# A one-core decoder trunk in split fp32: warm-up products ordered first, the bias table moved behind the first key product, the sub-norm's mean in another bank, and two output products fed tile by tile

## The chip, the cores and the metric

The kernel runs on one core of a Trainium2 chip. The metric is the time of one execution on the device, in microseconds (us). Several runs are timed, and one execution is recorded by the hardware profiler. Engine names: TensorE (PE, with PEld for its weight loads), VectorE (DVE), ScalarE (ACT), GpSimd (POOL) and SyncE (SP), which issues the DMA loads and stores.

## The reference

Two decoder layers over 512 tokens of width 1024, all in float32. What matters here, shortened:

```python
for i in range(2):
    hn = rmsnorm(h, norm_mix_g[i])
    # layer 0: 8 stick-breaking heads and 4 differential heads; layer 1: 16 dilated-window heads
    h = h + (even_mixer if i == 0 else odd_mixer)(hn, ...)
    hn = rmsnorm(h, norm_mlp_g[i])
    h = h + square(relu(hn @ w_mlp_up[i])) @ w_mlp_down[i]
    h = h + (p[i] @ w_ple_proj[i]) * sigmoid(rmsnorm(h, norm_ple_g[i]) @ w_ple_gate[i])
return rmsnorm(h, final_norm_g)

# differential head, in even_mixer
sc = q @ k.T * scale + t5_table[bucket(rel)]       # two maps per head, causal
attn = softmax(sc[0]) - lam * softmax(sc[1])       # lam from the four lambda vectors
o_d = rmsnorm(attn @ v, subln_g, 1e-5) * (1 - lambda_init)   # the "sub-norm", over 128 values
o = concatenate([o_sb, o_d]); return o @ w_out
```

## The kernel before

**Split products.** Activations lie transposed: h is eight tiles of 128 channels x 512 tokens. Each float32 operand is split into a high and a low half (ScalarE copies the high half, VectorE or GpSimd subtracts to get the low one), and `mm3` (L135 to L138) multiplies high x high, high x low and low x high. Where the page writes mm<-hi,wh or mm<-lo,wh, these are such products.

**Who sets the order.** The code is traced as one long list. A planner at compile time then lays it out on the engines: each engine gets a fixed order, chosen by a simulated clock and by the place in the list, and waits are put in for data and for buffers. On the chip an engine runs its own order strictly and stands still where its next instruction isn't ready. `order(later, earlier)` adds an edge to the plan between two instructions without a wait on the chip. Buffers are rotated by tags: `ps("mm")` has three PSUM banks, "sc" and "tp" two each, "pv" one (`PS_BUFS`). The tile "tmp" has one buffer, the raw weights two, the split weights three.

**Start.** L286 to L309: an activation table is loaded, ten products of the identity with itself (`WARM`, L291, 20 records, to a bank of "mm") are traced as warm-up, and SyncE loads the norm gains, the eight tiles of h and, in three pieces between them, the first weight block (the queries of the first group, `blk0`). Each tile of h is split with its gain (L178, L179) and so is each piece of the block (L308, L309).

**Mixer.** `project(g, cur)` makes queries, keys and values of a group; `attend` does the group's attention as a list of steps; `interleave` traces the steps of one group between the products of the next. Layer 0 takes the groups 2, 3, 0, 1, and 2 and 3 are the differential ones. In the first group `queries_keys` (L443) multiplies both query tiles at once, the eight tiles of h in turn, into two "sc" banks, and leaves the results there (`waiting`). Then it calls `prepare()` (L314), which builds the bias table: seven small loads into "bias" and "tmp" tiles, four small products L329 to "pv" and "tp" banks, four VectorE operations L331, four stores L332 to `urow` in device memory, from which `load_bias` (L511) reads each head's diagonal; it also makes the lambda factor. Then come the key block (load L114, splits L122 and L128) and its two products. After the first of them `statistics()` sums the squares of h (L237, L243), forms the mean with two products (L250, L251) and the reciprocal root (L206 to L212), and with it the held queries and then the keys are evicted (`evacuate`, L470 to L486).

**Attention.** A step scores one block of 128 queries (`scores`, L502, L503), adds the bias and takes the minimum (L519), exponentiates (L522), and with a lag transposes (L528), splits the transposed weights (L536, L537) and, once per head, multiplies with the values into the "pv" bank (`pv`, L547; evicted by L601 or L608). In a differential group `subnorm` follows two steps after each head: squares (L614, L615, L616), the mean over the head's channels by two products L618 and L619 into a "pv" bank, the reciprocal root (L206 to L212, of which L206 and L211 read that bank), and the scaling L621. There are two heads in each of two groups, so four sub-norms.

**Output.** `out_first` multiplies the first six of the eight head tiles with the output weights, beside the attention of the last group: eight sums, each of 18 products in a row into one "mm" bank, added to h by L658. The tiles are split by L175 and L176. Then the last two tiles follow, the MLP, and the per-layer embedding.

Of the kernel before, what the change touches and what calls it, by code (L numbers as in the profile page):

```python
# [19 lines left out]
P = 128  # L20
# [42 lines left out]
def trunk(  # L63
# [5 lines left out]
    nc = tc.nc  # L69
# [28 lines left out]
    def ps(tag):  # L98
        return psum.tile([P, S], F32, tag=tag, name=nm(tag), bufs=PS_BUFS[tag])
# [31 lines left out]
    def block(src, nk, n):  # L131
        raw = wload(src)
        return [wsplit(raw, i, nk, n) for i in range(src.shape[-1] // (nk * n))]

    def mm3(acc, lh, ll, rh, rl, start, stop):  # L135
        nc.tensor.matmul(acc, lh, rh, start=start, stop=False)  # L136
        nc.tensor.matmul(acc, lh, rl, start=False, stop=False)  # L137
        nc.tensor.matmul(acc, ll, rh, start=False, stop=stop)  # L138

# [5 lines left out]
    def lin_units(accs, ws, ahl, k0, nk, outer):  # L145
        pairs = [(i, k) for k in range(nk) for i in range(len(accs))] if outer else \
            [(i, k) for i in range(len(accs)) for k in range(nk)]
        for i, k in pairs:
            ah, al = ahl[k0 + k]
            mm3(accs[i], ws[i][0][:, k], ws[i][1][:, k], ah, al, k == 0, k == nk - 1)  # L150
            yield 2.0
# [31 lines left out]
    ident = const([P, P], "ident")  # L183
# [36 lines left out]
    def order(later, earlier):  # L220
        tc.add_manual_dep(
            later, earlier.name,
            mybir.DependencyInfo(mybir.DependencyClass.NoSync, mybir.DependencyReason.DATA),
            reason="activation tables")
# [63 lines left out]
    nc.scalar.preload_act_table_set("natural_log_exp_and_others")  # L288
    warm = ps("mm")
    for _ in range(WARM):  # L290
        nc.tensor.matmul(warm[:, 0:P], ident, ident, start=True, stop=True)  # L291
    norm = Norm(0, 0)
    raw0 = wpool.tile([P, 2 * KT * P], F32, tag="raw", name=nm("raw"), bufs=2)
    raw0v = raw0.rearrange("p (i k c) -> p i k c", i=2, k=KT)
# [73 lines left out]
    def mixer(layer, norm, nxt):  # L368
# [35 lines left out]
        def project(g, cur):  # L404
            kind = "dil" if layer else ("sb" if g < 2 else "diff")
            start = not first
            first.append(g)
            v = mpool.tile([P, QT, 512], F32R, tag="v", name=nm("v"), bufs=2)

            def values():  # L410
                raw = wload(next_block())
                banks = [ps(lead_in.pop(0)) if start else ps("mm") for _ in range(QT // 2)]
                accs = [b[:, c:c + 256] for b in banks for c in (0, 256)]
                for half in range(2):
                    wh, wl = wsplit(raw, half, 4, 256)
                    if half and "rcol" not in stat:
                        stat["rcol"] = tok_cols(stat["rstd"])
                    for t in range(QT):
                        for k in range(4):
                            ah, al = ahl[4 * half + k]  # L420
                            tk = slice(t * P, (t + 1) * P)
                            mm3(accs[t], ah[:, tk], al[:, tk], wh[:, k], wl[:, k],
                                half == 0 and k == 0 and t % 2 == 0, half == 1 and k == 3 and t % 2 == 1)
                            yield 1.0
                        if half == 1 and t % 2 == 1:
                            evacuate_values(t - 1, accs[t - 1])
                            evacuate_values(t, accs[t])

            def evacuate_values(t, acc):
                sc = stat["rcol"][:, t:t + 1]  # L430
                if kind == "diff":
                    src = acc
                    vh, vl = v[:, t, 0:256], v[:, t, 256:512]
                else:
                    src = acc.rearrange("p (a c) -> p a c", a=4)
                    vv = v[:, t, :].rearrange("p (a b c) -> p a b c", a=4, b=2)
                    vh, vl = vv[:, :, 0, :], vv[:, :, 1, :]
                nc.scalar.activation(vh, src, AF.Copy, scale=sc)
                nc.vector.scalar_tensor_tensor(vl, src, sc, vh.bitcast(F32), op0=ALU.mult, op1=ALU.subtract)

            heads = []

            def queries_keys():  # L443
                qscale = -0.5 * HD ** -0.5 if kind == "sb" else 0.5 * HD ** -0.5
                qk, waiting = [], []
                for isq in (True, False):
                    src = next_block()
                    lo_eng[0] = nc.vector if start else nc.gpsimd
                    blk = blk0 if isq and start and not layer else block(src, KT, P)
                    lo_eng[0] = nc.gpsimd  # L450
                    accs = [ps(lead_in.pop(0)) if start else ps("mm") for _ in range(2)]
                    if start and isq:
                        yield from lin_units(accs, blk, ahl, 0, KT, True)
                        waiting = accs
                        if not layer:
                            prepare()
                        continue
                    for i, acc in enumerate(accs):
                        yield from lin_units([acc], [blk[i]], ahl, 0, KT, False)
                        if waiting:  # L460
                            statistics()
                            for x, held in enumerate(waiting):
                                evacuate(True, x, held, qk, qscale)
                            waiting = []
                        evacuate(isq, i, acc, qk, qscale)

            def evacuate(isq, i, acc, qk, qscale):
                rstd = stat["rstd"]
                f = t2k("tmp")
                nc.vector.scalar_tensor_tensor(f, acc, qscale if isq else -0.5, rstd, op0=ALU.mult, op1=ALU.mult)  # L470
                lower, upper = slice(0, 64), slice(64, 128)
                if isq:
                    qq = []
                    for a, b in ((lower, upper), (upper, lower)):
                        q = mpool.tile([P, S], F32R, tag="qq", name=nm("qq"), bufs=5)
                        nc.scalar.activation(q[a], f[a], AF.Copy)
                        nc.vector.tensor_tensor(q[b], f[a], q[a].bitcast(F32), op=ALU.subtract)
                        qq.append(q)
                    qk.append(qq)
                else:  # L480
                    for s, (a, b) in enumerate(((lower, upper), (upper, lower))):
                        kl = klz[s][kl_i[0] % KLB]
                        kh = mpool.tile([P, S], F32R, tag="kh", name=nm("kh"), bufs=5)
                        nc.scalar.activation(kh[a], f[a], AF.Copy)
                        nc.scalar.activation(kh[b], f[a], AF.Copy)
                        nc.vector.tensor_tensor(kl[a], f[a], kh[a].bitcast(F32), op=ALU.subtract)  # L486
                        heads.append((qk[i][s], kh, kl))
                    kl_i[0] += 1
            cur.extend((g, kind, v, heads))
            if start:  # L490
                yield from queries_keys()
                yield from values()
            else:
                yield from values()
                yield from queries_keys()
# [55 lines left out]
        def attend(g, kind, v, heads):  # L551
# [59 lines left out]
            def subnorm(x):  # L611
                o = oT[2 * g + x]
                hi, rs, lo = t2k("tmp2", dtype=F32R), t2k("tmp2"), t2k("tmp2", dtype=F32R)
                nc.scalar.activation(rs, o, AF.Square)  # L614
                nc.scalar.activation(hi, rs, AF.Copy)  # L615
                nc.vector.tensor_tensor(lo, rs, hi.bitcast(F32), op=ALU.subtract)  # L616
                mp = ps("pv")
                nc.tensor.matmul(mp, ones_r, hi, start=True, stop=False)  # L618
                nc.tensor.matmul(mp, ones_r, lo, start=False, stop=True)  # L619
                rsqrt(rs, t2k("tmp2"), mp, SUBLN_EPS, eps_s, scale=float(D // P))  # L620
                nc.vector.scalar_tensor_tensor(o, o, gsub, rs, op0=ALU.mult, op1=ALU.mult)  # L621
# [30 lines left out]
        def out_first():  # L652
            ohl.extend(split_tile(oT[k]) for k in tiles[len(ohl):6])
            for c in range(4):
                for i, ws in enumerate(block(w_outa[layer, c], 6, P)):
                    acc = ps("mm")
                    yield from lin_units([acc], [ws], ohl, 0, 6, False)
                    nc.vector.tensor_tensor(h[2 * c + i], h[2 * c + i], acc, op=ALU.add)  # L658

        cur = []  # L660
# [360 lines left out]
```

## Time and profile before

| what | value |
|---|---|
| median of 3 runs | 1309.7 us (1309.18 to 1309.81) |
| profiled execution | 1309.79 us |
| its span, first to last instruction | 1308.0 us |
| granted TensorE clock, mean | 0.998 |
| TensorE busy | 1281.9 us (98%) |
| VectorE busy | 974.1 us (74%) |
| ScalarE busy | 686.3 us (52%) |
| GpSimd busy | 191.2 us (15%) |
| DMA | 133.20 MB, mean 102 GB/s |

A row of the timeline has the start in us, the duration, the engine, the line of the program, the operation, output <- inputs, the shapes and how many were merged; in brackets stands how long the engine stood idle before it and what released it. Matmul durations overlap, so the rate of products is read from the distance of their starts. A row of the waits has who waited for whom, the sum in us, how often, and the longest.

### The profile page before, as it was taken

The page shows a single profiled execution, that of the slowest core. Times are in us where ns is not written, and L with a number is a line of the kernel's source. Part 1 is how long each engine was busy: PE and PEld are TensorE (multiplying, and loading weights), DVE is VectorE, ACT ScalarE, POOL GpSimd, SP SyncE. Part 2 cuts the span into 40 slices and gives each one's busy share as a digit, 9 for nine tenths or more (in the row PEclk, how much of TensorE's full clock was granted, in tenths as well). Part 3 has the DMA queues.
Part 4 walks back from the last instruction along what each step waited for, and adds up shares of the span by engine and source line. Part 5 has one row for each costly group of instructions (what it writes and reads, how often), then busy time and mean ns, then how long its engine had stood idle before and what let it go on. Part 6 is the DMA issues. An engine that isn't in the chain of part 4 may idle for free.

```text
span 1308.0 us, 18566 instructions
## 1 busy us (share of the span) xinstructions
PE 1281.9 (98%) x7256; PEld 1116.8 (85%) x7256; DVE 974.1 (74%) x1623; ACT 686.3 (52%) x1117; POOL 191.2 (15%) x160
## 2 busy tenths in 40 slices
PE   7999999999999999999999999999999999999997
PEld 5978788888998989988889888788899898998876
DVE  7688898778848869845767777887785885994566
ACT  6666868554535334334456666765553443533344
POOL 2432444310000000000024333222000000000001
PEclk9999999999999999999999999999999999999999
DMA  6421323223232322323432222212223223232241
GB/s 214 136 82 49 122 89 137 89 84 110 86 108 97 103 93 96 129 97 107 151 114 95 83 89 79 68 57 93 100 97 121 73 97 129 71 124 97 97 145 65
DMA packets 28040, 133.20 MB, mean 102 GB/s; under 512 B 3312, under 2 KB 4048, under 8 KB 15280
## 3 DMA queue, kind: packets, MB, share of 16 engines
q1 hardware_dynamic: 27952, 132.01, 29.2%
q8 instruction: 57, 0.93, 0.3%
q14 instruction: 31, 0.25, 0.1%
HBM read 125.63 MB, written 6.37 MB: 101 GB/s over the span
## 4 chain that ended last, share of the span: by engine, by line
PE 86%; DVE 8%; ACT 3%; issue 1%; DMA 1%; SPq 0%; ACTq 0%; DVEq 0%
PE mm L137 13%; PE mm L136 13%; PE mm L138 13%; PE sc L137 5%; PE sc L138 5%; PE sc L136 5%; PE tp L138 5%; PE tp L137 5%; PE tp L136 5%; PE pv L138 3%; PE pv L137 3%; PE pv L136 3%; PE pv L547 2%; PE tp L528 2%; PE sc L502 1%; PE sc L503 1%
## 5 line engine op out<-in xcount | busy, mean ns | idle before, releaser
L122 ACT ACTIVATE wh<-raw 128x1024 fp32r<-128x1024 f32 (+1 forms) x168 | 173.5, 1037 | 225.3 <-PE mm L137 94.6
L126 POOL TENSOR_TENSOR wl<-raw,wh 128x512 fp32r<-128x512 f32 (+1 forms) x132 | 178.5, 1373 | 308.8 <-ACT wh L122 303.2
L136 PE MATMUL mm<-hi,wh 128*128 128x512 f32 x548 | 216.2, 395 | 1.0 <-ACT hi L175 0.6
L138 PE MATMUL mm<-hi,wl 128*128 128x512 f32 x548 | 214.3, 391 | 0.8 <-DVE wl L128 0.8
L137 PE MATMUL mm<-lo,wh 128*128 128x512 f32 x548 | 214.4, 391 | 0.2 <-DVE lo L176 0.2
L128 DVE TENSOR_TENSOR wl<-raw,wh 128x1024 fp32r<-128x1024 f32 x102 | 124.4, 1224 | 41.2 <-ACT wh L122 34.8
L138 PEld LDWEIGHTS mm<-hi,wl 128*128 128x128 f32 x548 | 102.9, 188 | 23.8 <-DVE wl L128 1.2
L136 PEld LDWEIGHTS mm<-hi,wh 128*128 128x128 f32 x548 | 103.0, 188 | 20.5 <-ACT wh L122 1.2
L137 PEld LDWEIGHTS mm<-lo,wh 128*128 128x128 f32 x548 | 103.0, 188 | 19.0 <-DVE lo L176 0.5
L522 ACT ACTIVATE e<-e,mn 128x128 f32<-128x128 f32 (+3 forms) x96 | 53.9, 562 | 66.3 <-DVE mn L519 65.9
L745 ACT ACTIVATE wh<-raw 128x1024 fp32r<-128x1024 f32 x48 | 50.7, 1056 | 69.8 <-PE tp L137 35.5
L136 PE MATMUL sc<-hi,wh 128*128 128x512 f32 x184 | 72.3, 393 | 6.4 <-ACT wh L308 6.4
L724 DVE TENSOR_TENSOR ul<-u,uh 128x1792 fp32r<-128x1792 f32 (+1 forms) x32 | 58.4, 1824 | 23.4 <-ACT uh L723 23.4
L723 ACT ACTIVATE uh<-u 128x1792 fp32r<-128x1792 f32 (+1 forms) x32 | 49.4, 1543 | 48.5 <-DVE u L719 48.2
L138 PE MATMUL mm<-uh,wl 128*128 128x256 f32 (+1 forms) x240 | 73.7, 307 | 0.0
L137 PE MATMUL mm<-ul,wh 128*128 128x256 f32 (+1 forms) x240 | 73.5, 306 | 0.0
L136 PE MATMUL mm<-uh,wh 128*128 128x256 f32 (+1 forms) x240 | 72.9, 304 | 0.0
L137 PE MATMUL sc<-lo,wh 128*128 128x512 f32 x184 | 72.2, 392 | 0.0
L138 PE MATMUL sc<-hi,wl 128*128 128x512 f32 x184 | 72.1, 392 | 0.0
L712 ACT ACTIVATE u<-u 128x512 f32<-128x512 f32 x64 | 39.4, 624 | 54.5 <-DVE u L711 54.5
L137 PE MATMUL mm<-wl,hi 128*128 128x256 f32 (+1 forms) x224 | 66.1, 295 | 0.5 <-DVE wl L128 0.5
L136 PE MATMUL mm<-wh,hi 128*128 128x256 f32 (+1 forms) x224 | 66.1, 296 | 0.0
(263 smaller groups left out, 3498.8 us busy)
## 6 DMA issues: line engine op xcount, KB each, us to landing
raw<-in_w_up_dram SPq DMA_DIRECT2D x32, 1024.0 KB, 4.9
raw<-in_w_down_dram SPq DMA_DIRECT2D x32, 1024.0 KB, 4.9
raw<-in_w_in_dram SPq DMA_DIRECT2D x23, 1024.0 KB, 4.9
raw<-in_w_gate_dram SPq DMA_DIRECT2D x8, 1024.0 KB, 4.9
bias<-urow SPq DMA_DIRECT2D x24, 256.0 KB, 3.9
raw<-in_w_outa_dram SPq DMA_DIRECT2D x8, 768.0 KB, 4.3
pj<-pjd SPq DMA_DIRECT2D x16, 256.0 KB, 4.4
h<-in_xT_dram SPq DMA_DIRECT2D x8, 256.0 KB, 5.6
```

Of the source, the lines that this page charges most:

```text
L122: nc.scalar.activation(hi, src, AF.Copy)
L126: nc.gpsimd.tensor_tensor(lo[:, kx], src[:, kx], hi[:, kx].bitcast(F32), op=ALU.subtract)
L128: nc.vector.tensor_tensor(lo, src, hi.bitcast(F32), op=ALU.subtract)
L136: nc.tensor.matmul(acc, lh, rh, start=start, stop=False)
L137: nc.tensor.matmul(acc, lh, rl, start=False, stop=False)
L138: nc.tensor.matmul(acc, ll, rh, start=False, stop=stop)
L522: nc.scalar.activation(e[:, 0:n], e[:, 0:n], AF.Exp, scale=-1.0, bias=mn, accum_out=s)
L528: nc.tensor.transpose(tp[:, j * P:(j + 1) * P], e[:, j * P:(j + 1) * P], ident)
L712: nc.scalar.activation(ui, ui, AF.Square, scale=0.5)
L723: nc.scalar.activation(uh[:, parts], u[:, parts], AF.Copy)
L724: nc.vector.tensor_tensor(ul[:, parts], u[:, parts], uh[:, parts].bitcast(F32), op=ALU.subtract)
L745: nc.scalar.activation(hi, src, AF.Copy)
```

## The change

Four edits. The first key or query product traced gets a planning edge behind the last warm-up product. `prepare()` is called later: not before the key block but after the first key product, the statistics and the evictions of both query tiles. The sub-norm's mean goes to a bank of "mm" instead of "pv". In `out_first` both sums of a weight block take their banks together, and in the first block (c = 0) the six tiles are taken in turn, three products for one sum and three for the other; the additions to h are traced after both sums.

```diff
@@ -132,8 +132,12 @@
+    warm_end = []
+
     def mm3(acc, lh, ll, rh, rl, start, stop):
-        nc.tensor.matmul(acc, lh, rh, start=start, stop=False)
+        mm = nc.tensor.matmul(acc, lh, rh, start=start, stop=False)
+        if warm_end:
+            order(mm.ins, warm_end.pop())
         nc.tensor.matmul(acc, lh, rl, start=False, stop=False)
         nc.tensor.matmul(acc, ll, rh, start=False, stop=stop)
@@ -288,7 +292,7 @@
     warm = ps("mm")
     for _ in range(WARM):
-        nc.tensor.matmul(warm[:, 0:P], ident, ident, start=True, stop=True)
+        warm_end[:] = [nc.tensor.matmul(warm[:, 0:P], ident, ident, start=True, stop=True).ins]
@@ -452,8 +456,6 @@
                     if start and isq:
                         yield from lin_units(accs, blk, ahl, 0, KT, True)
                         waiting = accs
-                        if not layer:
-                            prepare()
                         continue
                     for i, acc in enumerate(accs):
                         yield from lin_units([acc], [blk[i]], ahl, 0, KT, False)
@@ -462,6 +464,8 @@
                             for x, held in enumerate(waiting):
                                 evacuate(True, x, held, qk, qscale)
                             waiting = []
+                            if not layer:
+                                prepare()
                         evacuate(isq, i, acc, qk, qscale)
@@ -614,7 +618,7 @@
-                mp = ps("pv")
+                mp = ps("mm")
                 nc.tensor.matmul(mp, ones_r, hi, start=True, stop=False)
                 nc.tensor.matmul(mp, ones_r, lo, start=False, stop=True)
@@ -652,9 +656,10 @@
             for c in range(4):
-                for i, ws in enumerate(block(w_outa[layer, c], 6, P)):
-                    acc = ps("mm")
-                    yield from lin_units([acc], [ws], ohl, 0, 6, False)
+                blk = block(w_outa[layer, c], 6, P)
+                accs = [ps("mm") for _ in range(2)]
+                yield from lin_units(accs, blk, ohl, 0, 6, c == 0)
+                for i, acc in enumerate(accs):
                     nc.vector.tensor_tensor(h[2 * c + i], h[2 * c + i], acc, op=ALU.add)
```

## The prediction

> **What bounds the kernel now.** I read the page first (busy shares, then the chain that ended last), then the list of waits of TensorE, then the timeline of the stretches in which those waits lie.
>
> ```profile
> PE 1281.9 (98%) x7256; PEld 1116.8 (85%) x7256; DVE 974.1 (74%) x1623; ACT 686.3 (52%) x1117; POOL 191.2 (15%) x160
> ...
> PE 86%; DVE 8%; ACT 3%; issue 1%; DMA 1%; SPq 0%; ACTq 0%; DVEq 0%
> ```
>
> TensorE is busy 98% of the span and is 86% of the chain; VectorE (DVE) has 8% of it. So time can be saved only where TensorE stands still, runs at a slow clock, or does work that nobody needs. The waits say where it stands still:
>
> ```profile
> PE sc L136 <- ACT wh L308: 6.4, 1, 6.4
> PE pv L547 <- DVE tmp L211: 2.8, 2, 1.4
> ...
> PE mm L136 <- ACT hi L175: 0.6, 1, 0.6
> ```
>
> The longest is the first product's wait for its weights, which the change does not touch. The others that bear on the change are 2.8 us in two pieces on a PSUM bank that the sub-norm holds, and 0.6 us before an output product. So what the change can bring is a matter of microseconds in 1308.
>
> The timeline of the start shows work that is slow or useless rather than late:
>
> ```profile
> 1.11 0.29 POOL masks.py:199 TENSOR_SCALAR_AFFINE_SELECT ident<-ident 128x128 f32<-128x128 f32 x1
> ...
> 6.95 0.63 PE L137 MATMUL sc<-lo,wh 128*128 128x512 f32 x1
> ...
> 9.08 0.45 PE L136 MATMUL sc<-hi,wh 128*128 128x512 f32 x1
> 9.37 2.39 PE L291 MATMUL mm<-ident 128*128 128x128 f32 x20
> 11.52 0.47 PE L137 MATMUL sc<-lo,wh 128*128 128x512 f32 x1
> ...
> 20.70 0.39 PE L138 MATMUL sc<-hi,wl 128*128 128x512 f32 x1
> 21.02 1.03 PE L329 MATMUL pv<-prep,prep 32*16 32x512 f32 x2
> 22.32 0.50 PE L250 MATMUL tp<-e,ones_r 128*128 128x512 f32 x1
> 23.26 0.50 PE L136 MATMUL mm<-hi,wh 128*128 128x512 f32 x1 [0.45 <-ACT wh L122]
> ...
> 35.86 0.28 PE L136 MATMUL pv<-wh,hi 128*128 128x256 f32 x1
> ```
>
> Products 2 to 7 start 0.43 us apart ((9.08 - 6.95) / 5); after 11.52 they start 0.23 us apart (40 steps up to 20.70). So the clock rises near 9.08, some 2.7 us after TensorE's first instruction at 6.4. Then the ten warm-up products (20 records) run from 9.37 to 11.52: behind seven real products, when the clock is already up. They cost 2.15 us and warm nothing. Their operand, the identity, was there at 1.40.
>
> **Part 1: warm-up first.** TensorE is idle until 6.4, so the 20 records start at about 1.5. At the fast rate they take 2.15 us, at half of it 4.3; they end between 3.7 and 5.8, before the first weights are split at 6.4. They cost nothing: what hides them is the wait of 6.4 us. If that cover were gone, the price is at most the 2.15 us they cost now. The seven slow products gain 7 x 0.20 = 1.4 us and the moved records 2.15, together 3.55 us if data keeps up. It does not quite:
>
> ```profile
> 12.63 2.07 DVE L179 SCALAR_TENSOR_TENSOR lo<-h,gcols,hi 128x512 fp32r<-128x512 f32 x3
> ...
> 8.10 0.43 SPq L317 DMA_DIRECT2D prep<-in_t_table_dram  x1
> ...
> 14.33 0.82 SPq L114 DMA_DIRECT2D raw<-in_w_in_dram  x2
> ...
> DMA to landing us min/median/max: 5.0/6.0/6.9
> ...
> 14.34 0.72 ACT L178 ACTIVATE hi<-h,gcols 128x512 fp32r<-128x512 f32 x1 [0.58 <-DMA h<-in_xT_dram]
> ...
> 22.17 1.99 ACT L122 ACTIVATE wh<-raw 128x1024 fp32r<-128x1024 f32 x2
> ...
> 24.50 2.34 DVE L128 TENSOR_TENSOR wl<-raw,wh 128x1024 fp32r<-128x1024 f32 x2
> ```
>
> The query products take the tiles of h in turn, six products each. The low halves of tiles 4 to 6 are made from 12.63 on, 0.69 us each, so the first is there at 13.32; from 6.4 the 24 products of the first four tiles need 5.5 us and leave 1.4 us for waits on their own halves. After 13.32 there are 23 products, 5.3 us, and the block ends at 18.6 (tile 7, whose high half starts at 14.34, is in time). Now it ends at 20.93. Gain 2.3 us; ends 1.0 (another half us at each of three tiles) and 3.55.
>
> [...]
>
> **Part 2: the bias table behind the first key product.** Now the seven small loads (first at 8.10) stand in SyncE's queue ahead of the key weights, issued at 14.33, and the key split is behind the statistics on ScalarE (22.17). In the change the key load takes the place of the load at 8.10. The two 1 MB loads issued from 14.33 on, 0.4 us apart, landed 5.0 and 6.9 us after issue, so they are served in line, 2.3 us each: the key weights come 2.3 us behind the last tile of h (there at 14.34), at about 16.6.
>
> Two ScalarE splits of 1.0 us and two VectorE splits of 1.17 us follow, among the squares. First high half about 18, first low half about 19.4. So the key products can begin at 18.6, against 23.26. From 20.93 to 35.86 TensorE now has 48 products (11.0), the two of the statistics (0.46) and the four small table products (21.02 to 22.32, 1.3): 12.8 of 14.9 us, 2.1 idle. The small products move back and still cost their 1.3. Of the idle time I keep 1.1: 0.4 for the first low half, 0.7 because the statistics' products now follow the first key product and their sum is delayed on VectorE by the two key splits (2.3 us). Key products end at 18.6 + 12.8 + 1.1 = 32.5; gain of both parts 35.86 - 32.5 = 3.4 us. Ends: 0 (the key split still planned behind the statistics, and the small products in the way later; a loss would need a key load issued after 14.33, and nothing new stands ahead of it) and 3.55 + 2.1 = 5.65; I take 3.4, from the data rows.
>
> What is moved, queue by queue. SyncE: seven loads go behind one key load (1 MB, 2.3 us); the value load waits for its buffer as now. The four stores of the table wait for VectorE's four small operations, and the bias loads for the stores; the bias is first used behind the first scores, 30 us after the table's products at 21.02. Those four operations leave VectorE's queue in front of the low-half split. The lambda load shares a one-buffer tile with the query and key evictions; if it gets that only behind both queries, the first key eviction is held for a load, less than the 5.0 us of the 1 MB ones. That lies in a slack:
>
> ```profile
> 28.20 0.95 DVE L212 SCALAR_TENSOR_TENSOR rstd<-e,rstd 128x512 f32<-128x512 f32 x1
> ...
> 38.68 0.69 DVE L486 TENSOR_TENSOR klz<-tmp,kh 64x512 fp32r<-64x512 f32 x1 [0.61 <-ACT kh L484]
> ...
> 51.04 0.28 PE L502 MATMUL sc<-kh,qq 128*128 128x256 f32 x1
> ```
>
> The norm is ready at 29.15, the first heads at 39.4, their scores start at 51.04 and would start near 47.6, 8 us after the heads. Both delays fit. So the whole attention stage starts 3.4 us earlier, and its weight loads with it.
>
> **Part 3: the sub-norm's mean in a general bank.** There is one "pv" bank. The sub-norm's mean holds it until VectorE's L211, and the next head's value product waits:
>
> ```profile
> 85.67 0.69 DVE L537 TENSOR_TENSOR ptl<-tp,pth 128x512 fp32r<-128x512 f32 x1
> ...
> 87.84 0.47 PE L547 MATMUL pv<-pth,v 128*128 128x512 f32 x1 [1.40 <-DVE tmp L211]
> 88.14 0.40 PE L547 MATMUL pv<-ptl,v 128*128 128x512 f32 x1
> 88.38 0.56 PE L547 MATMUL pv<-pth,v 128*128 128x512 f32 x2
> ...
> 91.76 0.57 ACT L601 ACTIVATE o<-pv 128x512 f32<-128x512 f32 x1
> ...
> 93.69 0.69 DVE L616 TENSOR_TENSOR tmp<-tmp,tmp 128x512 fp32r<-128x512 f32 x1 [1.77 <-ACT tmp L615]
> ...
> 94.44 0.50 PE L619 MATMUL pv<-tmp,ones_r 128*128 128x512 f32 x1
> ...
> 102.55 0.39 PE L502 MATMUL sc<-kh,qq 128*128 128x256 f32 x1 [1.07 <-DVE mn L519]
> ```
>
> L537, the operand of that product, is ready at 86.4; without the bank the product starts 1.4 us earlier, and as much at the second of the two waits. What is late next: TensorE runs on to the next sub-norm's product L619, which at 94.44 already waits for L616, and that hangs on L601, whose row names no wait: it stood in ScalarE's queue behind the key copies, and was not held by the value product. With that order kept, all of the gain is lost at L619; with L601 moved ahead of the copies, up to 2.8 is kept. After it stands a wait for VectorE at 102.55. I take 0.8, nearer to the kept order; ends 0 and 2.8 (a loss is the fourth rival). Cost: a general bank is held for over six us (below).
>
> **Part 4: first two output products tile by tile.**
>
> ```profile
> 847.00 0.39 PE L136 MATMUL mm<-hi,wh 128*128 128x512 f32 x1
> ...
> 851.37 0.49 PE L136 MATMUL mm<-hi,wh 128*128 128x512 f32 x1 [0.57 <-ACT hi L175]
> 852.10 0.50 PE L137 MATMUL mm<-lo,wh 128*128 128x512 f32 x1 [0.23 <-DVE lo L176]
> ```
>
> In the last layer the first product's sixth tile (15 products after 847.00) waits for its high and its low half, there at 852.1. In turn over two banks 30 products stand ahead of it, until 853.8: the wait goes. 0.57 + 0.23 = 0.8 us, ends 0 and 0.8. TensorE is the bound there, so it is kept; a loss is excluded while the bank count suffices. In the first layer no such wait is listed: nothing. Two banks now finish together; the third carries the next product for 4 us (18 x 0.23) while two additions of 0.7 us free them.
>
> **Sum.** 3.4 + 0.8 + 0.8 = 5.0 us off the profiled execution's 1309.79 (span 1308.0 and 1.8 around it; 0.1 above the median of the runs): 1304.8. Ends of the terms: 0 and 9.25 off, so 1309.8 and 1300.5.
>
> **Rivals.** 1. The front gain is lost: the attention of the first group is paced by VectorE and ScalarE, or the planned order keeps the key split late. For it: the norm is ready at 29 either way, and VectorE holds TensorE up as late as 102.55. Against: the scores start 11 us after their heads. Then only parts 3 and 4 stand, 1.6 off: 1308.2.
>
> 2. The clock is still slow at 6.4: the warm-up is done early, or TensorE's pause before 6.4 lets it fall. Then the first seven products stay slow and 1.4 us of the front go: 1306.2. Against it: after 1.40 us without work, at 87.84, products of 512 columns are again 0.24 us apart (88.14 to 88.38). [...]
>
> 3. More: L601 moves ahead and both sub-norm waits are kept, the front reaches 4.5: 4.5 + 2.8 + 0.8 = 8.1 off, 1301.7.
>
> 4. Slower: three general banks no longer do. The mean takes one from about 94 to the end of L211 at 100.84, the values' products need two at once, and a key sum waits for its eviction:
>
> ```profile
> 95.66 0.69 DVE L470 SCALAR_TENSOR_TENSOR tmp<-mm,rstd 128x512 f32<-128x512 f32 x1 [1.28 <-PE mm L138]
> ...
> 95.47 0.28 PE L136 MATMUL mm<-wh,hi 128*128 128x256 f32 x1
> ...
> 98.33 0.28 PE L136 MATMUL mm<-wh,hi 128*128 128x256 f32 x1
> ...
> 100.17 0.67 DVE L211 SCALAR_TENSOR_TENSOR tmp<-pv,tmp 128x512 f32<-128x512 f32 x1
> ```
>
> If the values' second bank has to be the mean's, TensorE stops from 98.33 to 100.84, 2.5 us, at each of four sub-norms: 10.0 - 4.2 (the sum without part 3) = 5.8 slower, 1315.6. It decides from 1.05 us per sub-norm. Against it: the key sum's bank is free at 96.35, 2 us before it is needed.
>
> **How the numbers follow.** The forecast 0.57 (own range 1302.5 to 1306.8), rival 1 0.17, rival 2 0.07, rival 3 0.11, rival 4 0.08. The time predicted is the likeliest, 1304.8. The range for 8 in 10 is 1301.2 to 1308.6: it drops rival 4 and the far end of rival 3. A change under 0.2% (2.6 us) can't be told from none here: faster, below 1307.1: 0.57 + 0.07 + 0.11 = 0.75; same, 0.17; slower 0.08.
>
> **What will show it.** Part 1: the warm-up rows before 6.36 and query products 0.23 apart from the first; the last near 18.6. Part 2: the key load issued near 8.1, first key product near 18.6, first value product near 32.5, first scores near 47.6. Part 3: no wait of L547 on L211; then L619 or L502 waits longer, or L601 stands ahead of the key copies. Part 4: no wait on L175 and L176 near 847. It is wrong if the stretch from 60 to 145 gives the front gain back, or if waits on a general bank appear: the planned order of all queues is made anew, and a wait of one or two us anywhere in the attention stages weighs as much as any part of this.

## The result: slower by 4 us instead of faster by 5

| kernel | median, us | lowest to highest | ratio to before, 95% |
|---|---|---|---|
| before | 1310.16 (8 runs) | 1309.18 to 1312.15 | |
| after | 1314.16 (8 runs) | 1313.43 to 1316.63 | 1.0029 [1.0019, 1.0040] |

The medians differ by 4.0 us, 0.3%, and the interval of the ratio lies above 1. The forecast was 1304.8, in a range that ended at 1308.6. The page of the changed kernel, busy time and the shares of the chain that ended last:

```profile
PE 1287.3 (98%) x7256; PEld 1119.7 (85%) x7256; DVE 973.0 (74%) x1623; ACT 686.1 (52%) x1117; POOL 188.7 (14%) x160
...
PE 84%; DVE 9%; ACT 5%; issue 1%; DMA 1%; SPq 0%; POOL 0%; ACTq 0%; DVEq 0%; POOLq 0%
```

Its span is 1313.3 us and its granted clock 0.996, against 0.998 before. TensorE is busy 5.4 us longer than before (1287.3 against 1281.9) with the same number of instructions: some of its work ran at a slower clock. In the chain, VectorE and ScalarE gained what TensorE lost: new waits.

To find where time is won and lost, I numbered the products that `mm3` makes in order of their start (6360 in each trace) and took the difference of the n-th starts, after minus before. The columns name the start of that product in before; the first is the first key product, the last is the last product. The two profiled executions took 1315.09 and 1309.79 us, so this table adds up to 5.3 us and not to the 4.0 of the medians.

| kernel | 23.3 | 36.0 | 58.2 | 144.6 | 179.0 | 258.0 | 1299.4 |
|---|---|---|---|---|---|---|---|
| after | -4.1 | -3.2 | -1.0 | -0.1 | +3.2 | +5.1 | +5.3 |

So the front gains 3.2, against 3.4 forecast, and three places take it away and more: the start of the attention (36 to 58, and the rest until 70), a place between 145 and 179, and one between 179 and 258. From 258 to the end the difference grows by only 0.2.

**The front comes out as forecast.** Timeline of TensorE, after:

```profile
1.46 3.93 PE L295 MATMUL mm<-ident 128*128 128x128 f32 x20 [1.46 <-POOL ident masks.py:199]
5.72 0.50 PE L138 MATMUL sc<-hi,wh 128*128 128x512 f32 x1 [0.33 <-ACT wh L312]
6.06 0.40 PE L141 MATMUL sc<-lo,wh 128*128 128x512 f32 x1
6.29 0.42 PE L142 MATMUL sc<-hi,wl 128*128 128x512 f32 x1
...
19.18 0.39 PE L138 MATMUL mm<-hi,wh 128*128 128x512 f32 x1
...
32.62 0.28 PE L138 MATMUL pv<-wh,hi 128*128 128x256 f32 x1
...
47.80 0.28 PE L506 MATMUL sc<-kh,qq 128*128 128x256 f32 x1
...
50.32 0.28 PE L142 MATMUL mm<-wh,lo 128*128 128x256 f32 x1
52.58 0.39 PE L506 MATMUL sc<-kh,qq 128*128 128x256 f32 x1 [1.99 <-DVE mn L523]
```

The warm-up is done at 5.7, the first product is followed at the fast rate, the key products follow the last query product without a pause at 19.18, the first value product stands at 32.62 (forecast 32.5), and the first scores at 47.80 (forecast 47.6). Then the second scores wait for 1.99 us, on a minimum that VectorE (L523) has not taken yet.

**Why that minimum is late.** Timelines of SyncE's queue (SPq, the issue of DMAs) and of VectorE, after:

```profile
30.91 1.84 SPq L336 DMA_DIRECT2D urow<-prep  x4
36.03 1.29 SPq L515 DMA_DIRECT2D bias<-urow  x3
37.78 0.33 SPq L329 DMA_DIRECT2D tmp<-in_lambdas_dram  x1
...
35.26 2.49 DVE L481 TENSOR_TENSOR qq<-tmp,qq 64x512 fp32r<-64x512 f32 x2 [0.70 <-ACT qq L480]
...
41.63 0.83 DVE L337 TENSOR_TENSOR tmp<-tmp 128x128 f32<-128x128 f32 x1 [2.46 <-DMA tmp<-in_lambdas_dram]
...
42.82 0.69 DVE L474 SCALAR_TENSOR_TENSOR tmp<-mm,rstd 128x512 f32<-128x512 f32 x1
...
52.24 0.28 DVE L523 CUSTOM_DVE_ANT_0 e<-sc,bias 128x128 f32<-128x128 f32 x1
```

The lambda load (L329) was traced into the one-buffer tile "tmp". In the changed order both query evictions come first, so it gets the tile only behind them and is issued at 37.78, between the bias loads. VectorE stands still for 2.46 us until it lands, and the first key eviction (L474) comes at 42.82; the four heads, the values and the minimum follow on the same queue, and L523 comes at 52.24.

**The sub-norm.** Timeline of TensorE at the end of the first group:

```profile
93.58 0.51 PE L622 MATMUL mm<-tmp,ones_r 128*128 128x512 f32 x1 [1.23 <-ACT tmp L619]
94.31 0.50 PE L623 MATMUL mm<-tmp,ones_r 128*128 128x512 f32 x1 [0.22 <-DVE tmp L620]
```

No wait on the "pv" bank remains, and the product of the mean waits 1.23 and 0.22 us for ScalarE and VectorE instead, as the kept order of part 3 said. Then, at the fourth sub-norm (rows of TensorE, ScalarE and VectorE in order of time):

```profile
143.22 0.50 PE L622 MATMUL mm<-tmp,ones_r 128*128 128x512 f32 x1 [1.20 <-ACT tmp L619]
143.94 0.50 PE L623 MATMUL mm<-tmp,ones_r 128*128 128x512 f32 x1 [0.22 <-DVE tmp L620]
...
145.07 1.05 ACT L122 ACTIVATE wh<-raw 128x1024 fp32r<-128x1024 f32 x1
...
147.96 1.76 DVE L490 TENSOR_TENSOR klz<-tmp,kh 64x512 fp32r<-64x512 f32 x1
149.65 0.68 DVE L215 SCALAR_TENSOR_TENSOR tmp<-mm,tmp 128x512 f32<-128x512 f32 x1
...
150.38 0.50 PE L138 MATMUL mm<-wh,wh 128*128 128x512 f32 x1 [1.84 <-DVE tmp L215]
...
151.52 0.63 PE L141 MATMUL mm<-wl,wh 128*128 128x512 f32 x1
151.95 0.63 PE L142 MATMUL mm<-wh,wl 128*128 128x512 f32 x1
...
154.51 0.47 PE L142 MATMUL mm<-wh,wl 128*128 128x512 f32 x1
```

The mean is written to a general bank from 143.22 on. The reciprocal root that empties the bank (L210 to L215) stands in both queues among other work: a weight copy (L122) on ScalarE, two of the heads' low halves (L490) on VectorE. The bank comes free at 150.33, and the product of the per-layer embedding, for which it was the next of three, waits 1.84 us. After it the products start 0.43 us apart, not 0.23, from 151.5 to 154.5: the clock is at half rate. Wait and clock together are the 3.3 us from -0.1 to +3.2.

**The output products in the first layer**, timeline of TensorE:

```profile
226.22 0.50 PE L138 MATMUL mm<-hi,wh 128*128 128x512 f32 x1 [0.51 <-ACT wh L122]
...
227.53 0.50 PE L142 MATMUL mm<-hi,wl 128*128 128x512 f32 x1 [0.58 <-POOL wl L126]
```

Two waits for the high and the low half of a weight tile, which before does not have there.

### The profile page after: what moved, and what is told of

It is laid out like the page before. It is cut to its first block, busy times and chain, and to the rows that moved or that the text cites. A ratio compares the mean times of both kernels' runs of the same rounds, so it can differ in the third digit from the quotient of the medians.

```text
span 1313.3 us, 18566 instructions
## 1 busy us (share of the span) xinstructions
PE 1287.3 (98%) x7256; PEld 1119.7 (85%) x7256; DVE 973.0 (74%) x1623; ACT 686.1 (52%) x1117; POOL 188.7 (14%) x160
## 4 chain that ended last, share of the span: by engine, by line
PE 84%; DVE 9%; ACT 5%; issue 1%; DMA 1%; SPq 0%; POOL 0%; ACTq 0%; DVEq 0%; POOLq 0%
PE mm L142 13%; PE mm L141 13%; PE mm L138 13%; PE sc L141 5%; PE sc L142 5%; PE sc L138 5%; PE tp L141 5%; PE tp L142 5%; PE tp L138 5%; PE pv L142 3%; PE pv L141 3%; PE pv L138 3%; PE pv L551 2%; PE tp L532 2%; PE sc L506 1%
## 5 line engine op out<-in xcount | busy, mean ns | idle before, releaser
L122 ACT ACTIVATE wh<-raw 128x1024 fp32r<-128x1024 f32 (+1 forms) x168 | 173.3, 1036 | 229.3 <-PE mm L141 94.7
```

The costliest lines, as they stand in the source:

```text
L122: nc.scalar.activation(hi, src, AF.Copy)
```

## Experiments

Each kernel was timed in five rounds with the kernel before on the same chip. The medians of before in the three sessions were 1310.04, 1309.98 and 1309.97. The differences are between starts of the n-th products as above, from one profile each; at the same pause the clock fell in one profile and not in another (see the end), and one fall is worth up to 1.7 us (half of the 3.41 us that a slow stretch lasts in after), so a single row can be off by that much against the medians.

| kernel | median, us | ratio to before, 95% | 23.3 | 36.0 | 58.2 | 144.6 | 179.0 | 258.0 | 1299.4 |
|---|---|---|---|---|---|---|---|---|---|
| e1_lambda_own | 1310.32 | 1.0003 [0.9994, 1.0012] | -4.4 | -3.6 | -3.6 | -3.6 | -1.8 | -0.2 | -0.7 |
| e2_mean_pv | 1311.69 | 1.0010 [1.0001, 1.0019] | -4.4 | -3.6 | +0.1 | +0.1 | +0.1 | +2.0 | +2.3 |
| e3_turn_last | 1313.05 | 1.0023 [1.0014, 1.0031] | -4.3 | -3.6 | +0.2 | +0.2 | +3.5 | +3.8 | +3.3 |
| e4_all_three | 1306.61 | 0.9974 [0.9963, 0.9984] | -4.2 | -3.4 | -3.4 | -3.4 | -3.3 | -3.3 | -3.2 |
| p1_warm | 1311.48 | 1.0011 [1.0002, 1.0020] | +0.2 | +1.6 | +1.6 | +1.8 | +1.8 | +1.8 | +1.7 |
| p1_fill | 1310.17 | 1.0000 [0.9991, 1.0009] | +0.7 | -0.3 | -0.3 | -0.1 | -0.1 | -0.1 | -0.1 |
| p2_lam | 1307.97 | 0.9984 [0.9975, 0.9993] | -1.1 | -0.9 | -0.9 | -1.0 | -1.1 | -1.1 | -1.0 |
| p12_lam | 1306.44 | 0.9973 [0.9964, 0.9983] | -4.4 | -3.7 | -3.7 | -3.6 | -3.6 | -3.6 | -3.4 |
| p3_mean | 1313.12 | 1.0021 [1.0013, 1.0030] | 0.0 | +1.6 | +1.6 | +1.6 | +5.0 | +5.0 | +5.3 |
| e5_no_warm | 1306.67 | 0.9971 [0.9960, 0.9982] | -4.4 | -3.9 | -3.9 | -3.5 | -3.5 | -3.5 | -4.0 |

The first four start from after, and each takes back one of the three suspects, the fourth all of them.

**e1_lambda_own**: the lambda load gets a buffer of its own.

```diff
-        lamt = t2k("tmp")[:, 0:4 * HD].rearrange("p (j c) -> p j c", j=4)
+        lamt = t2k("tmp2")[:, 0:4 * HD].rearrange("p (j c) -> p j c", j=4)
```

> The changed kernel with one edit: the lambda load gets a tile of another tag (tmp2) in place of the one-buffer tile tmp that the query and key evictions use. Theory: the 3.2 us won at the start were lost because the first key eviction waited for the lambda load (issued at 37.8 behind the queries' evictions and three bias loads, landed at 41.6, first key eviction at 42.8 against 36.0 before). Then the first key eviction comes near 38, no wait of 2 us before the second pair of scores, first scores near 47.5 and the gain of about 3 us is still there at 145 us: 2.2 to 3.3 us faster than the changed kernel, 1310.9 to 1312. Rival: VectorE and ScalarE pace the attention of the first two groups whatever the front does (the norm is ready at 31.0, 1.9 us later than before): key eviction earlier, but the lead is gone by 95 us all the same, 0 to 0.7 us faster than the changed kernel.

```profile
13.55 0.35 SPq L329 DMA_DIRECT2D tmp<-in_lambdas_dram  x1
...
37.58 0.69 DVE L474 SCALAR_TENSOR_TENSOR tmp<-mm,rstd 128x512 f32<-128x512 f32 x1
```

(SyncE's queue and VectorE.) The load now stands among the small loads at 13.55, the first key eviction comes at 37.58 instead of 42.82, the wait of the second scores is gone, and the front's lead goes through unbroken to 144.6. In the medians 1314.16 - 1310.32 = 3.8 us: the largest of the three, and more than the 2.2 to 3.3 expected. The 1.84 us on the bank are still there, at 146.93, and the waits at the output products too (0.49 and 0.59), so the lead of 3.6 is all but eaten by 258. In this profile the clock did not fall behind the 1.84 us (products 0.23 apart, mean granted clock 0.998); its execution, 1309.02, is the fastest of the eleven.

**e2_mean_pv**: the sub-norm's mean goes back to the "pv" bank.

```diff
-                mp = ps("mm")
+                mp = ps("pv")
```

> The changed kernel with the sub-norm's mean back in the one pv bank. Theory: the mean's general bank costs the 3.3 us that appear at 148 us (a product of the per-layer embedding waits 1.84 us for the bank, and TensorE's clock is at half rate from 151.5 to 154.5 after it), and gains nothing at 86 and 137 us because TensorE waits for the next sub-norm's squares instead. So 2.5 to 3.5 us faster than the changed kernel, about 1310.9, with two waits of 1.4 us before the value products back and none at 148. Rival: the wait at 148 only moves, because the embedding's products come on full banks anyway, and the two waits come back on top: within 1 us of the changed kernel.

The list of waits and the timeline of TensorE:

```profile
PE pv L551 <- DVE tmp L215: 2.8, 2, 1.4
...
52.17 0.38 PE L506 MATMUL sc<-kh,qq 128*128 128x256 f32 x1 [1.98 <-DVE mn L523]
...
55.88 0.41 PE L141 MATMUL mm<-wl,hi 128*128 128x256 f32 x1
56.10 0.41 PE L142 MATMUL mm<-wh,lo 128*128 128x256 f32 x1
```

Nothing is lost between 144.6 and 179.0. The wait on the "pv" bank is back, 2.8 us in two pieces as before, and costs nothing in the end, because without it TensorE waits further on. Against after 1314.16 - 1311.69 = 2.5 us. This profile shows another drop of the clock, behind the 1.98 us pause of the second scores (256-column products 0.21 apart where they are 0.12 apart otherwise, until 56.3); in after the same pause has none. So the late minimum costs 3.0 us in the profile of after and 3.7 here, where the clock falls too.

**e3_turn_last**: only the last layer takes the tiles in turn.

```diff
-                yield from lin_units(accs, blk, ohl, 0, 6, c == 0)
+                yield from lin_units(accs, blk, ohl, 0, 6, layer == 1 and c == 0)
```

> The changed kernel with the tiles taken in turn in the last layer's first output block alone. Theory: in the first layer the order in turn needs the second half of the weight block two products after the first, and TensorE waits 0.51 us for its high and 0.58 us for its low half at 226 us; the first layer's loss is 1.6 us, so 1.3 to 1.9 us faster than the changed kernel, about 1312.5. Rival: the stretch is paced by the attention steps between the products, and the waits come elsewhere: within 0.5 us.

From 179.0 to 258 only 0.3 us is lost, where after loses 1.9; in the medians 1.1 us, less than the 1.3 to 1.9 expected. The intervals of this kernel and of after overlap, so for the time alone this is the weakest of the three; the two waits at 226 to 228 are gone in its trace.

**e4_all_three**: e1, e2 and e3 together.

```diff
-        lamt = t2k("tmp")[:, 0:4 * HD].rearrange("p (j c) -> p j c", j=4)
+        lamt = t2k("tmp2")[:, 0:4 * HD].rearrange("p (j c) -> p j c", j=4)
-                mp = ps("mm")
+                mp = ps("pv")
-                yield from lin_units(accs, blk, ohl, 0, 6, c == 0)
+                yield from lin_units(accs, blk, ohl, 0, 6, layer == 1 and c == 0)
```

> The three edits of the other runs together on the changed kernel. Theory: the three losses add, 3.0 + 3.3 + 1.6 = 7.9 us off 1314.2, so about 1306.3, 3 to 4.5 us faster than the kernel before. Rival: the front's lead runs into VectorE in the attention of the differential groups and the three give back only what the change lost: 1309.5 to 1311, as before.

7.55 us less than after; the single effects sum to 3.8 + 2.5 + 1.1 = 7.4. Each interval above reaches some 1.2 us to either side, so it is partly luck that the two numbers meet to 0.2 us. The three causes account for the loss, and what is left is the front's gain, constant from product to product up to the last layer. This kernel beats both.

The next kernels start from before and put single parts in.

**p1_warm**: part 1 alone (the planning edge behind the last warm-up product; nothing else).

> The kernel before with the warm-up order alone. Theory: the query products end about 2.1 us earlier (near 18.8 in place of 20.9), but the first key product still waits for the key split, which stands behind the statistics on ScalarE at 22 us, so the lead is lost at 23.3: 0 to 0.5 us faster, within noise of the kernel before. Rival: the lead of 2 us lives on because TensorE's later products are what ends last: about 2 us faster, 1308.

A miss: it is 1.5 us slower. Timeline of TensorE:

```profile
23.44 0.50 PE L138 MATMUL mm<-hi,wh 128*128 128x512 f32 x1 [2.68 <-ACT wh L122]
...
24.70 0.74 PE L142 MATMUL mm<-hi,wl 128*128 128x512 f32 x1 [0.53 <-DVE wl L128]
25.24 0.63 PE L138 MATMUL mm<-hi,wh 128*128 128x512 f32 x1
25.67 0.63 PE L141 MATMUL mm<-lo,wh 128*128 128x512 f32 x1
...
28.22 0.40 PE L141 MATMUL mm<-lo,wh 128*128 128x512 f32 x1
28.45 0.40 PE L142 MATMUL mm<-hi,wl 128*128 128x512 f32 x1
```

The query block starts earlier and ends 1.5 us earlier (its last product starts at 19.19, in before at 20.70), but the key load still stands behind the table's loads, so TensorE runs into pauses of 2.68 and 0.53 us (before: 0.45 and 0.8). The first key product is no earlier (+0.2), and then the clock is at half rate: products 0.43 apart until 28.2. The lag at 36.0 is 1.6.

**p3_mean**: part 3 alone (the one line of e2 in the other direction, in before).

> The kernel before with the sub-norm's mean in a general bank and nothing else; on TensorE the order is the one before but for the bank and for two scores moved ahead of products near 148 us. Theory: 1.8 us slower for the wait for the bank at 148 us, up to 3.4 where the clock drops after it, and nothing gained at 86 and 137 us: 1311.8 to 1313.4. Rival: the loss at 148 came of the other edits' shift of the queues, and this edit alone keeps part of the two waits of 1.4 us: 1308.5 to 1310.

It costs 3.1 us in the medians, more than in the whole change. The place is the same (TensorE):

```profile
152.15 0.68 PE L136 MATMUL mm<-wh,wh 128*128 128x512 f32 x1 [1.85 <-DVE tmp L211]
152.63 0.63 PE L137 MATMUL mm<-wl,wh 128*128 128x512 f32 x1
153.05 0.63 PE L138 MATMUL mm<-wh,wl 128*128 128x512 f32 x1
```

1.85 us on the reader of the mean, and half rate behind it. (The 1.6 us that this profile lags at 36.0 are slow products from 25.8 to 29.2, ahead of any sub-norm, behind pauses of 0.44 and 0.81 us; before has 0.45 and 0.80 there and no slow products. Its own time, 1315.05, is 1.9 above its median.)

**p12_lam**: parts 1 and 2 with the lambda load in its own buffer; neither part 3 nor part 4.

```diff
-        nc.tensor.matmul(acc, lh, rh, start=start, stop=False)
+        mm = nc.tensor.matmul(acc, lh, rh, start=start, stop=False)
+        if warm_end:
+            order(mm.ins, warm_end.pop())
...
-        lamt = t2k("tmp")[:, 0:4 * HD].rearrange("p (j c) -> p j c", j=4)
+        lamt = t2k("tmp2")[:, 0:4 * HD].rearrange("p (j c) -> p j c", j=4)
...
-                        if not layer:
-                            prepare()
...
+                            if not layer:
+                                prepare()
```

> The kernel before with the warm-up order and the later bias table, the lambda load in its own tile; mean and output products as before. Theory: the lead of 3.2 to 3.6 us that the traces show from the first value product on is the whole gain of the run with all three edits, so this one is as fast as that within 0.7 us: 1306 to 1307.3. Rival: the in-turn order of the last layer, which removes waits of 0.8 us near 850, is a real part of it: 0.7 to 1 us slower than that run, about 1307.5.

1306.44 against 1306.61 of e4, which has part 4 in the last layer on top: the medians show nothing of part 4's 0.8. The two profiles can't decide it, because in both the clock falls at 842 (in e4 products of 512 columns start 0.43 apart from 844.58 on; the mean granted clock is 0.997 in both), and behind that fall p12_lam has no wait at the output product either. Where the clock does not fall there, the difference to before drops between 842 and 900 by 0.54 to 0.59 us in the three kernels with part 4 in the last layer (e1, e3, e5) and by at most 0.01 in the three without (p1_warm, p1_fill, p2_lam). So part 4 gains some 0.55 us in such an execution, and none in e4's.

**e5_no_warm**: e4 without warm-up products (`WARM = 0`).

> The kernel with all three edits without the ten warm-up products. Theory: the gain at the start came from taking the warm-up out of the middle of the query products, not from warming: the first seven products run at half rate (0.43 us in place of 0.23 apart, 1.4 us), but the low half of the fifth tile of h, ready at 13.3 us, holds the block's end anyway, so 0 to 0.6 us slower than with warm-up, about 1306.9. Rival: the clock's rise is worth its 1.4 us: 1.2 to 1.8 us slower, about 1308.1.

```profile
5.27 0.80 PE L138 MATMUL sc<-hi,wh 128*128 128x512 f32 x1 [5.27 <-ACT wh L312]
5.87 0.63 PE L141 MATMUL sc<-lo,wh 128*128 128x512 f32 x1
...
8.00 0.63 PE L138 MATMUL sc<-hi,wh 128*128 128x512 f32 x1
```

The first product comes at 5.27 and the next six start 0.43 apart, at half rate, yet at 36.0 the lead is that of e4, and the time is the same (1306.67 and 1306.61). In these medians the warm-up products earn nothing even at the front; what part 1 gains is that they no longer stand in the middle.

The last two ask what made p1_warm lose, and what part 2 does without part 1.

**p1_fill**: p1_warm, and identity products between the last query product and the first key product.

```diff
+FILL = 18
...
+                            fill = ps("mm")
+                            for _ in range(FILL):
+                                mm = nc.tensor.matmul(fill[:, 0:P], ident, ident, start=True, stop=True)
+                                order(mm.ins, last_mm[0])
```

> Before with the warm-up products ordered first (as p1_warm, 1311.5), and 18 identity products of 128x128 written to a spare general bank between the last query product and the first key product, so that TensorE is not idle while it waits for the key split. Theory (the loss of part 1 alone is the clock that drops after the pauses of 2.68 and 0.53 us, some 1.5 us): the seven products at half rate go, and the time is 1309.5 to 1310.5, 1 to 2 us under p1_warm. Rival (the loss lies in the key transfer, which lands no earlier, and in the order behind it): 1311 to 1313, no better than p1_warm, or worse by the filler's own time.

```profile
18.72 4.18 PE L463 MATMUL mm<-ident 128*128 128x128 f32 x36
...
24.01 0.50 PE L139 MATMUL mm<-hi,wh 128*128 128x512 f32 x1
24.34 0.40 PE L142 MATMUL mm<-lo,wh 128*128 128x512 f32 x1
24.58 0.39 PE L143 MATMUL mm<-hi,wl 128*128 128x512 f32 x1
```

The identity products (18, as 36 records) run from 18.72 to 22.9, across the stretch in which p1_warm stood still. The first key product is 0.57 us later than in p1_warm (24.01 and 23.44), yet the products go on 0.23 apart, and 12 products further on the kernel is 1.8 us ahead of p1_warm (-0.8 and +1.0 against before). 1310.17 against 1311.48, 1.3 us gained by adding work that nobody needs: the loss of p1_warm against before is the clock. The late key transfer, the rival, explains why nothing is gained, not why it is lost: the key products start no earlier here.

**p2_lam**: p12_lam without the planning edge of the warm-up.

> Before with the table's preparation loads behind the key load and the lambda load in a buffer of its own, as in p12_lam (1306.4), but the warm-up products stay where before has them. Theory (the gain of the front is the key split being there when the query products end; the warm-up products in the middle cost their own time, some 2 us, on top): first key product about 1.5 to 2 us earlier than before, time 1307.8 to 1308.6. Rival A (the key transfer alone sets the front): as p12_lam, 1306.2 to 1307. Rival B (without the reordering nothing is gained): 1309.5 to 1310.5.

```profile
9.42 3.54 PE L291 MATMUL mm<-ident 128*128 128x128 f32 x20
...
21.90 0.39 PE L138 MATMUL sc<-hi,wl 128*128 128x512 f32 x1
22.13 0.39 PE L136 MATMUL mm<-hi,wh 128*128 128x512 f32 x1
```

The warm-up again stands behind seven slow products, in the middle; the query block ends at 22.1, and the key products follow at once. 2.0 us gained in the medians (1.0 in the profile, whose own time of 1308.75 is 0.8 above the median), against 3.5 with the edge. So with the key weights early the edge is worth 1.5 us, and without them it costs 1.5: parts 1 and 2 hang on each other.

## Why the prediction was wrong

**Part 1 and part 2, the front: right to 0.2 us.** Forecast 3.4 us; p12_lam gives 3.5 (1309.98 - 1306.44). Key load forecast at 8.1, issued at 7.82 in after; first value product forecast at 32.5, found at 32.62. Part of that is luck, for two errors cancel: the query block gave way to the keys 0.6 us later than forecast (19.18 for 18.6), and from there to the first value product it took 13.4 us instead of 13.9. Rival 2, a slow clock at 6.4, did not come (after 5.72 the products of after start at 6.06 and 6.29); no row of before shows a clock that falls behind a pause, and the falls that the runs showed came at other places (see the end). e5_no_warm, whose first products are slow, shows that it would have cost nothing: "The seven slow products gain 7 x 0.20 = 1.4 us" was no gain of its own, since the query block waits for its tiles further on.

**The lambda load: the step that failed first.** The prediction saw that it would come behind both queries and that the first key eviction would be held. It set the delay under 5.0 us; it is 42.82 - 37.58 = 5.2. And it measured the slack at the wrong place: "8 us after the heads" is the distance of the first scores to the first head. But the eviction heads a queue. Behind it on VectorE stand four heads, the values and then the minimum of those scores; TensorE meets that minimum at the second scores, 2.6 us behind the first (53.67 and 51.04 in before). There the slack was gone: the wait of 1.99 us takes most of it, holds of 0.3 and 0.4 us at the scores of 62.36 and 68.73 take most of the rest, and 3.8 us are lost (e1). Rival 1 forecast that the front's gain would be lost in this stage, but not for this reason: with the load in a tile of its own VectorE and ScalarE don't hold the attention up (e1 keeps its 3.6 us to 144.6).

**Part 3: the kept order was right, the price of the bank was not.** All of the gain at the "pv" bank was lost at the mean's product, as written (forecast 0.8, nearer to 0: it is 0). The loss was looked for at one place, the values' second bank at 98.3, where it does not occur, and given 0.08. It occurs once, at the fourth sub-norm, where the embedding products run through the same three banks; 7.1 us of holding (143.22 to 150.33) instead of the "over six" written, at 1.84 us plus 1.5 of the clock. The step that failed is the choice of place: the first group's rows were read, and the same bank was not followed to the fourth sub-norm.

**Part 4: "in the first layer no such wait is listed: nothing" failed.** That before has no wait there says only that nothing can be gained. In turn, the first product of the second sum comes 3 products behind the first one's, where it came 18 behind, so both tiles of the weight block have to be split at the start; they were not, 0.51 and 0.58 us. In the last layer the waits went as forecast; of the 0.8 us some 0.55 came in the profiles in which the clock stayed up there, and nothing shows in the medians.

**Sum.** 3.5 from the front, less 3.8, 2.5 and 1.1 (of single edits taken back), is 3.9 slower; measured 4.0, closer than the single numbers are good for.

## What to carry to other kernels

A transfer or a small job that is moved needs its buffer looked up as well: a one-buffer tile shared with the evictions turned a load that nobody waits for into 5 us at the head of VectorE's queue. Slack has to be followed down that queue to the next instruction on which the bounding engine waits, not only to the first consumer of the delayed result. And a chain that takes a bank from a pool is charged at every place where the pool is busy, so each of its instances has to be looked at.

## What the runs showed of the hardware

TensorE's clock fell to half rate after pauses of 0.4 to 2.7 us, and not every time. It fell after 2.68 + 0.53 us (p1_warm), after 1.84 or 1.85 us (after, e3_turn_last and p3_mean, but not e1_lambda_own), and after 1.98 us (e2_mean_pv and e3_turn_last, but not after, whose pause was 1.99 at the same place). In p3_mean it also fell after 0.44 and 0.81 us, where before has 0.45 and 0.80 and no fall. No fall was seen after the single pauses of 1.40 us. In the last layer, where a wait of 1.3 us and one of 0.5 us follow each other closely, it fell in after, e2_mean_pv, e4_all_three, p12_lam and p3_mean, and not in the others. The mean granted clock of the profiles goes with this: 0.998 in the five without a fall (before, e1_lambda_own, e5_no_warm, p1_fill, p2_lam), 0.997 in the three with one (p1_warm, e4_all_three, p12_lam), 0.995 or 0.996 in the four with more.

In after the granted clock is 0.50 for 3.41 us at each of its two falls (151.27 to 154.68 and 851.00 to 854.41); in p1_warm the products are 0.43 apart from 25.24 to 28.22. Half of 3.41 us is 1.7 us, the estimate of what one fall can cost. The stretches at full clock before, between and behind the two falls of after are 146.77 us long (from 4.49, where the record of the clock begins), 696.32 and 453.97: within 0.1 us 43, 204 and 133 times 3.413. Four stretches of after; a row has the stretch, its length, TensorE's busy time (with the number of products), the granted clock, and the share and rate of the DMA engines:

```profile
147.85:151.27 3.42, 1.57 (x11) 1.00 0.37 43
151.27:154.68 3.41, 3.41 (x10) 0.50 0.90 312
48.87:52.28 3.41, 1.73 (x15) 1.00 0.01 2
52.28:55.69 3.41, 3.11 (x25) 1.00 0.00 0
```

The pause of 1.84 us lies in the first row, and the second is at half rate. The pause of 1.99 us lies across 52.28, 1.68 us of it in the third row and 0.30 in the fourth, and the clock stays up. So the length of a pause alone did not decide whether the clock fell. What did was not shown: no run varied the length or the place of a pause by itself, and the ends of products are modelled. Whether a pause of 2 us would cost up to another 1.7 us could not be told ahead from these runs.
